# One quarter of x transposed by the DMA crossbar behind two of four FFNs, one sum of output weights by an accumulating load, and single stores, in a two-layer hybrid trunk

## The chip, the cores and the metric

The program runs on one core of one Trainium2 chip. The metric is the device time of one execution in microseconds (us), the median of three; lower is better.

## The reference

x is 512 x 1024 in float32. Two layers are run over it, each an FFN with weight 1/2, a mixer, and a second FFN with weight 1/2, and each behind an RMSNorm; a last RMSNorm gives the output. The first layer's mixer is recurrent (convolution, gates, a scan), the second's is a chunked spatial gating unit.

```python
def swiglu(x, w_in, w_out):
    g, u = jnp.split(x @ w_in, 2, axis=-1)          # w_in 1024 x 5632
    return (jax.nn.silu(g) * u) @ w_out             # w_out 2816 x 1024

h = x
for i in range(DEPTH):                               # DEPTH = 2
    h = h + 0.5 * swiglu(rms_norm(h, ffn1_norm[i]), ffn1_w_in[i], ffn1_w_out[i])
    h = h + mixer_i(rms_norm(h, mix_norm[i]))
    h = h + 0.5 * swiglu(rms_norm(h, ffn2_norm[i]), ffn2_w_in[i], ffn2_w_out[i])
return rms_norm(h, final_norm)
```

The program's order is thus FFN 1, recurrent mixer, FFN 2, FFN 3, spatial mixer, FFN 4, final norm.

## The kernel before, in words

**Products.** Every large matrix product is done in seven block products in place of eight (P1, P2, P5, P6, P3, P7, Q4: Strassen's scheme in Winograd's form). The left matrix is cut into quarters A11, A12, A22, A21, and the products take these and their sums S1 to S4 (`LEFT` names which). Each float32 operand is split into a high and a low part (`hi`, `lo`, for weights `whi`, `wlo`): ScalarE (ACT) copies the high part, VectorE (DVE) subtracts it from the value, and TensorE (PE) makes three matmuls, high by high, low by high and high by low (L465 to L467).

**Steps.** The list `subs` holds one entry for each product and each chunk of its inner dimension, some 570 in all. The last loop of `trunk` goes through them in order; at step i it splits the weights of step i+3 (`Sub.split`, L176 on), runs what was hooked to step i (`hook(n, phase, fn)`; the phases in order are pre, mid, rest, then the step's matmuls, then end and late), issues loads of weights (`load_more`) and issues the step's matmuls. A full step has 12 matmuls of 128 x 512. All engines work through their instructions in this written order, each at its own pace.

**Weights.** A load goes out on SP's queue (L140) into one of ten buffers (`raw`). Where a product needs a sum of two blocks of weights, the second block is either loaded into a buffer of its own (`tile`) and added by VectorE (`tt(self.raw.v, ...)`, in `Sub.add`), or added by an accumulating DMA on POOL's queue (`Raw.add`, L143). `Sub(..., then=block)` asks for such an accumulating load right behind the split, so that a later product finds the next sum in the same buffer. In an FFN's output products (`out_blocks` with `chain=True`), the products P1, P5, P6 and Q4 of a chunk share one buffer in this way. Before the change P6's own sum is always made with a second buffer and VectorE.

**The order of an FFN's output products** is the table `CHAIN`: 42 steps, product and chunk, such as `P25 P54 P62 Q40 Q41 P63 P55 P64 Q42 Q43 P65`. Chunk 0 has one block row of weights (128 x 512, six matmuls), chunks 1 to 5 have two.

**The norm behind an FFN.** When the last P2 is done, the quarter A11 of x (rows 0 to 255, columns 0 to 511) has its final value, and `BlockNorm.quarter("A11")` is called at that step, n. It squares the quarter for the mean, and it brings the quarter's four blocks of columns, in two groups of two, into transposed form for the next product. Before the change this is `Group.stage`: at the end of step n+2 eight 128 x 128 transposes run on TensorE (L276, `e<-ident,x`, four a group), then ScalarE takes each group out of PSUM with the norm's gain as the scale (two 128 x 256 copies), and the group is split into hi and lo (one 128 x 512 ACTIVATE, one 128 x 512 TENSOR_TENSOR). The A12, A22 and A21 quarters follow later in the same way. `BlockNorm.rest` hooks the sums S2, S4, S3 to the next product's first steps.

**The crossbar.** `Group.send` (L306 on) transposes the FFN's inner activations without TensorE: ScalarE writes the float32 values as two 16-bit planes (`pl`, two ACTIVATEs), SP issues one DMA transpose (L317), and ScalarE merges the two transposed planes into float32 (`a<-dt`, one ACTIVATE). `Group.rows` (L385 on) is the same for a quarter of x; it keeps the gains apart (`self.gain`), so that later steps multiply by them. Before the change nothing calls it.

**The end.** `FinalNorm` scales the last tiles of x and stores them. Row tiles 2 and 3 are stored together, one DMA of 512 KB per half of the columns (L1114), row tiles 0 and 1 singly (L1116).

Of the kernel before, what the change touches and what calls it, by code (L numbers as in the profile page):

```python
# [14 lines left out]
P = 128  # L15
# [10 lines left out]
V_F1, V_MIX, V_F2, V_CW, V_CB, V_GA, V_GX, V_LAM, V_SB = 0, 16, 32, 48, 80, 88, 96, 104, 112  # L26
# [31 lines left out]
def trunk(ctx: ExitStack, tc: tile.TileContext, a: dict, out: bass.AP):  # L58
    nc = tc.nc
# [19 lines left out]
    def bank(name="ps"):  # L79
        return mmp.tile([P, 512], F32, tag="mm", name=nm(name))  # L80
# [130 lines left out]
    def raw_of(src, shape, *plus):  # L211
        raws.append(Raw(src, shape, *plus))
        return raws[-1]
# [25 lines left out]
    X = cp.tile([P, TT, D], F32, tag="x", name="x")  # L239
# [178 lines left out]
    def seven(block, cuts, left, w, posts, order=None, own=False, apart=False, joined=None, opening=None,  # L418
              also=None, chain=False):

        bk, raw, held = {}, {}, []  # L430
        banks = dict(BANK, Q4=("Q", True)) if apart else BANK

        def mm_of(prod, ci):
            name, fresh = banks[prod]
            pairs = cuts[ci]

            def mm(sub):
                if fresh and ci == 0:
                    for s in range(2):
                        bk[name, s] = bank(name)[:, :w]  # L440
                if prod == joined and ci == len(cuts) - 2:
                    held.extend((sub, q, i) for q, i in enumerate(pairs))
                    return
                if opening and prod == "P1":
                    qs = list(enumerate(pairs))
                    for n, (q, i, m, s) in enumerate([(q, i, m, s) for q, i in qs for m in range(3) for s in range(2)]
                                                     if ci == 0 else
                                                     [(q, i, m, s) for m in range(3) for q, i in qs for s in range(2)]):
                        if n == (4 if ci else 6):
                            opening[ci]()  # L450
                        nc.tensor.matmul(bk[name, s], left(prod, i, s)[m == 1], (sub.lo if m == 2 else sub.hi)[:, q, :],
                                         start=(i, m) == (0, 0), stop=(i, m) == (cuts[-1][-1], 2))
                    for s in range(2 * ci):
                        posts[prod](s, bk[name, s])
                    return
                for s in range(2):
                    ps = bk[name, s]
                    k = {} if fresh else dict(skip_group_check=True)
                    if prod == joined and also is not None and ci == len(cuts) - 1:
                        also(s, ps)  # L460
                    for sb, q, i in (held if prod == joined else []) + [(sub, q, i) for q, i in enumerate(pairs)]:
                        zh, zl = left(prod, i, s)
                        wh, wl = sb.hi[:, q, :], sb.lo[:, q, :]
                        end = i == cuts[-1][-1]
                        nc.tensor.matmul(ps, zh, wh, start=fresh and i == 0, stop=False, **k)  # L465
                        nc.tensor.matmul(ps, zl, wh, start=False, stop=False, **k)  # L466
                        nc.tensor.matmul(ps, zh, wl, start=False, stop=end, **k)  # L467
                    if ci == len(cuts) - 1 and prod in posts:
                        posts[prod](s, ps)
            return mm  # L470

        kept = (0, 1) if joined else (0, 1, 2)
        order = order or [(p, ci) for p in ORDER for ci in range(len(cuts))]

        def far(ci):
            return own and order.index(("P6", ci)) - order.index(("P5", ci)) >= 4

        def again(ci):
            return own and order.index(("P5", ci)) - order.index(("P1", ci)) >= 6

        for prod, ci in order:
            if opening and (prod, ci) == ("P5", 0):
                opening[2]()

            def new(k, n, plus=None, wait=2):
                b = lambda k, n: block(k, n, cuts[ci])
                return raw_of(b(k, n), [P, len(cuts[ci]), w], plus and b(*plus), wait)

            tile = then = tile_then = None
            if chain:  # L490
                if prod == "P1" and ci in kept:
                    r, then = new(0, 0), block(0, 1, cuts[ci])
                    raw[11, ci] = r
                elif prod == "P5" and ci in kept:
                    r = raw[11, ci]
                elif prod in ("P1", "P2"):
                    r = new(int(prod == "P2"), 0)
                elif prod == "P5":
                    r = raw[11, ci] = new(0, 0, (0, 1))
                elif prod == "P6":  # L500
                    r, tile, then = raw[11, ci], new(1, 1), block(1, 0, cuts[ci])
                elif joined and prod == "P7" and ci in (4, 5):
                    r, tile = new(0, 1), new(1, 1)
                    raw[33, ci] = tile
                elif joined and prod == "P3" and ci in (4, 5):
                    r = raw[33, ci]
                elif joined and prod in ("P3", "P7"):
                    r = new(1, 1) if prod == "P3" else new(0, 1, (1, 1))
                elif prod == "P3":
                    r, then = new(1, 1), block(0, 1, cuts[ci])  # L510
                    raw[33, ci] = r
                else:
                    r = raw[33 if prod == "P7" else 11, ci]
            elif prod == "P1":
                r = raw[11, ci] = new(0, 0)
                if again(ci):
                    then = block(0, 1, cuts[ci])
            elif prod == "P2":
                r = new(1, 0)
            elif prod == "P5":  # L520
                if again(ci):
                    pass
                elif own:
                    raw[11, ci] = new(0, 0, (0, 1))
                    if far(ci):
                        then = block(1, 1, cuts[ci])
                else:
                    tile = raw[12, ci] = new(0, 1)
                    tile_then = block(1, 1, cuts[ci])
                r = raw[11, ci]  # L530
            elif prod == "P6" and far(ci):
                r, then = raw[11, ci], block(1, 0, cuts[ci])
            elif prod == "P6":
                r, tile, then = raw[11, ci], new(1, 1), block(1, 0, cuts[ci])
                raw[22, ci] = tile
            elif prod == "P3":
                r = new(1, 1) if far(ci) else raw[22, ci]
            elif prod == "P7":
                r = raw[12, ci] if not own else new(0, 1, (1, 1), 2 + ci if far(ci) else 2)
            else:  # L540
                r = raw[11, ci]
            subs.append(Sub(r, mm_of(prod, ci), None, tile, then, tile_then))
        return order


    def xt(t, n):
        return X[:, t, n * 512 : (n + 1) * 512]
# [169 lines left out]
    def out_blocks(w, k0, groups, scale, norm=None, order=None, own=False, soon={}, swap=False, p2_lag=0, chain=False, rows=None):  # L717
# [71 lines left out]
        def q4(s, ps):  # L789
# [3 lines left out]
            if not ends:  # L793
                final(2 + s, 0, "A21", s)

        at0, ends = len(subs), hasattr(norm, "last")
        order = seven(block, cuts, left_of(lambda: [gs[i] for i in range(len(n))]), 512,
                      dict(P1=p1, P2=p2, P5=p5, P6=p6, P3=p3, P7=p7, Q4=q4), order, own, True,
                      "P3" if ends else None, also=norm.gather if ends else None, chain=chain)
# [243 lines left out]
    class FinalNorm:  # L1043
# [63 lines left out]
            self.store(t, n, queue)  # L1107

        def store(self, t, n, queue=None):
            c = slice(n * 512, (n + 1) * 512)  # L1110
            if t == 2:
                return
            if t == 3:
                nc.sync.dma_start(out=out[0, 2 * P :, c].rearrange("(t p) c -> p t c", p=P), in_=X[:, 2:, c])  # L1114
                return
            (queue or nc.sync).dma_start(out=out[0, t * P : (t + 1) * P, c], in_=xt(t, n))  # L1116

        def piece(self, t, n):
            at = now[0]
# [447 lines left out]
    last = FinalNorm()  # L1567
    ffn(a["ffn1_w_in"][0], a["ffn1_w_out"][0], TileNorm(V_MIX))
    recurrent(a["rec_w_in"][0], a["rec_w_out"][0], BlockNorm(V_F2, True, wait=("A12",)))
    ffn(a["ffn2_w_in"][0], a["ffn2_w_out"][0], BlockNorm(V_F1 + 8, True))  # L1570
    ffn(a["ffn1_w_in"][1], a["ffn1_w_out"][1], BlockNorm(V_MIX + 8, True))
    spatial(a["sg_w_in"][0], a["sg_w_out"][0], BlockNorm(V_F2 + 8, True, late=True, wait=("A22",)))
    ffn(a["ffn2_w_in"][1], a["ffn2_w_out"][1], last)
    hook(len(subs) - 40, "late", last.load)
# [202 lines left out]
```

## Time and profile before

| what | value |
|---|---|
| median of 3 runs | 1564.46 us (1564.36 to 1564.46) |
| the profiled execution's own time | 1564.85 us |
| its span in the profile | 1563.1 us |
| TensorE busy | 1555.5 us, 7317 matmuls |
| VectorE busy | 1309.0 us |
| ScalarE busy | 1180.0 us |
| POOL (GpSimd) busy | 242.2 us |
| granted TensorE clock | 0.999 |
| read from HBM | 282.39 MB, 182 GB/s over the span |

The span counts from the program's first to its last instruction; the profiled execution's own time is 1.8 us more. The chain of waits is the list of pieces, each of which had to end before the next could begin, followed back from the end. A row of the timeline gives the start and the length of an instruction, its engine, line and tiles, and in brackets how long the engine had stood idle before it and for whom. A row of the view by windows gives each engine's busy time in a stretch, the granted clock, the mean busy share of the 16 DMA engines and the GB/s.

### The profile page before, as it was taken

Reading aid. Unit: us, or ns where it says so; the run is one execution under the profiler, and the core shown is the slowest. Engines: PE = TensorE matmul, PEld = TensorE weight load, DVE = VectorE, ACT = ScalarE, POOL = GpSimd, SP = SyncE. Lnnn points to the kernel's source line nnn. Section 1 sums busy time; section 2 is a strip of 40 time slices with the busy share of each in tenths; the row PEclk is TensorE's granted clock in tenths of the full one; section 3 lists DMA queues with packets and bytes.
Section 4 is the critical chain, followed back from the end, with each engine's and each line's share of the span. In section 5 each row is a group of like instructions: output and inputs, shape, how many; then the busy total and the mean of one; then the engine's idle time right before and its main releaser. Section 6 shows DMA issues by size and latency. Waiting matters only on the chain.

```text
span 1563.1 us, 21027 instructions
## 1 busy us (share of the span) xinstructions
PE 1555.5 (100%) x7317; PEld 1321.1 (85%) x7317; DVE 1309.0 (84%) x1771; ACT 1180.0 (75%) x1765; POOL 242.2 (15%) x217
## 2 busy tenths in 40 slices
PE   9999999999999999999999999999999999999998
PEld 7888888898888998888889988888888889888886
DVE  6977789978999877789887877898878997777998
ACT  7877886658778868886677788876786877778856
POOL 2111112200020111112211111122211111111120
PEclk9999999999999999999999999999999999999999
DMA  9888899943396888889978788989877869888994
GB/s 315 187 189 196 188 222 229 221 136 107 106 226 144 190 195 200 201 212 231 226 178 183 192 203 189 223 224 228 222 190 201 202 136 218 196 212 188 232 235 133
DMA packets 262426, 308.95 MB, mean 198 GB/s; under 512 B 104896, under 2 KB 142896, under 8 KB 262320
## 3 DMA queue, kind: packets, MB, share of 16 engines
q1 hardware_dynamic: 208464, 209.23, 45.6%
q0 software_dynamic: 52064, 96.54, 36.6%
q10 hardware_dynamic: 1792, 1.84, 0.5%
q8 instruction: 57, 0.93, 0.2%
q14 instruction: 49, 0.40, 0.1%
HBM read 282.39 MB, written 2.10 MB: 182 GB/s over the span
## 4 chain that ended last, share of the span: by engine, by line
PE 100%; DVE 0%; ACT 0%; issue 0%
PE A L465 15%; PE A L466 15%; PE A L467 15%; PE C L466 9%; PE C L465 8%; PE C L467 8%; PE B L466 4%; PE B L465 4%; PE B L467 4%; PE r L232 2%; PE r L231 2%; PE r L230 2%; PE Q L467 2%; PE Q L465 2%; PE Q L466 2%; PE p L939 1%
## 5 line engine op out<-in xcount | busy, mean ns | idle before, releaser
L92 DVE TENSOR_TENSOR wlo<-raw,whi 128x1024 fp32r<-128x1024 f32 (+2 forms) x567 | 651.2, 1152 | 211.1 <-ACT whi L101 204.3
L101 ACT ACTIVATE whi<-raw 128x1024 fp32r<-128x1024 f32 (+2 forms) x567 | 564.6, 1001 | 248.8 <-DVE raw L92 87.6
L465 PE MATMUL A<-whi,hi 128*128 128x512 f32 (+1 forms) x1104 | 421.0, 381 | 0.0
L467 PE MATMUL A<-wlo,hi 128*128 128x512 f32 (+1 forms) x1104 | 419.4, 380 | 0.0
L466 PE MATMUL A<-whi,lo 128*128 128x512 f32 (+1 forms) x1104 | 419.3, 380 | 0.0
L465 PEld LDWEIGHTS A<-whi,hi 128*128 128x128 f32 x1104 | 207.3, 188 | 35.9 <-ACT c L101 0.9
L467 PEld LDWEIGHTS A<-wlo,hi 128*128 128x128 f32 x1104 | 207.3, 188 | 35.7
L466 PEld LDWEIGHTS A<-whi,lo 128*128 128x128 f32 x1104 | 207.3, 188 | 35.3 <-DVE lo L92 0.3
L465 PE MATMUL C<-whi,hi 128*128 128x512 f32 (+1 forms) x608 | 231.5, 381 | 0.0
L466 PE MATMUL C<-whi,lo 128*128 128x512 f32 (+1 forms) x608 | 231.4, 381 | 0.0
L467 PE MATMUL C<-wlo,hi 128*128 128x512 f32 (+1 forms) x608 | 231.3, 380 | 0.0
L143 POOL DMA_DIRECT2D raw<-in_ffn_w_in_dram x100 | 120.8, 1210 | 710.2 <-DVE raw L92 270.8
L92 DVE TENSOR_TENSOR raw<-raw,raw 128x1024 f32<-128x1024 f32 (+2 forms) x116 | 132.8, 1145 | 1.1
L466 PEld LDWEIGHTS C<-whi,lo 128*128 128x128 f32 x608 | 114.2, 188 | 20.3 <-DVE lo L92 0.6
L465 PEld LDWEIGHTS C<-whi,hi 128*128 128x128 f32 x608 | 114.2, 188 | 19.9
L467 PEld LDWEIGHTS C<-wlo,hi 128*128 128x128 f32 x608 | 114.1, 188 | 20.0
L143 POOL DMA_DIRECT2D raw<-in_ffn_w_out_dram x70 | 81.2, 1186 | 320.6 <-DVE wlo L92 192.5
L92 DVE TENSOR_TENSOR lo<-a,hi 128x512 fp32r<-128x512 f32 (+1 forms) x188 | 121.7, 654 | 0.8 <-ACT hi L101 0.7
L101 ACT ACTIVATE hi<-a 128x512 fp32r<-128x512 f32 (+1 forms) x188 | 110.8, 596 | 14.2 <-DVE a L92 12.8
L466 PE MATMUL B<-whi,lo 128*128 128x512 f32 (+1 forms) x304 | 115.8, 381 | 0.0
L465 PE MATMUL B<-whi,hi 128*128 128x512 f32 (+1 forms) x304 | 115.7, 381 | 0.0
L467 PE MATMUL B<-wlo,hi 128*128 128x512 f32 (+1 forms) x304 | 115.6, 380 | 0.0
(185 smaller groups left out, 1919.9 us busy)
## 6 DMA issues: line engine op xcount, KB each, us to landing
raw<-in_ffn_w_in_dram SPq DMA_DIRECT2D x143, 512.0 KB, 5.6
raw<-in_ffn_w_out_dram SPq DMA_DIRECT2D x98, 512.0 KB, 5.6
raw<-in_ffn_w_in_dram POOLq DMA_DIRECT2D x76, 512.0 KB, 7.5
raw<-in_ffn_w_out_dram POOLq DMA_DIRECT2D x58, 512.0 KB, 8.3
raw<-in_ffn_w_in_dram SPq DMA_DIRECT2D x48, 384.0 KB, 4.9
raw<-in_sg_w_in_dram SPq DMA_DIRECT2D x20, 512.0 KB, 7.9
raw<-in_ffn_w_in_dram POOLq DMA_DIRECT2D x24, 384.0 KB, 6.5
raw<-in_rec_w_in_dram SPq DMA_DIRECT2D x16, 512.0 KB, 5.1
```

Source lines behind the costliest of these rows:

```text
L92: nc.vector.tensor_tensor(out=o, in0=x, in1=y, op=op)
L101: nc.scalar.activation(out=o, in_=x, func=f, **k)
L143: nc.gpsimd.dma_start(out=self.v, in_=src, accum_op=ALU.add)
L230: nc.tensor.matmul(ps, wh, xh, start=start, stop=False)
L231: nc.tensor.matmul(ps, wh, xl, start=False, stop=False)
L232: nc.tensor.matmul(ps, wl, xh, start=False, stop=stop)
L465: nc.tensor.matmul(ps, zh, wh, start=fresh and i == 0, stop=False, **k)
L466: nc.tensor.matmul(ps, zl, wh, start=False, stop=False, **k)
L467: nc.tensor.matmul(ps, zh, wl, start=False, stop=end, **k)
L939: nc.tensor.matmul(bank_of(half, s), z, (sub.lo if m == 2 else sub.hi)[:, q, :], start=left[2] == "2" and (h, q, m) == (0, 0, 0), stop=lef ...
```

## The change

Three edits are made at once.

1. The norms behind FFN 2 and FFN 3 get `cross={"A11": ...}`. The quarter A11 then goes by `Group.rows` in place of `Group.stage`: planes and DMA transpose at steps n+2 and n+3 behind FFN 2 (n+1 and n+2 behind FFN 3), the merge at steps n+6 and n+7, the split behind the merge with the gains (two 128 x 256 ACTIVATEs and two 128 x 256 SCALAR_TENSOR_TENSORs a group). The sum S2 of the next product then is two 128 x 256 SCALAR_TENSOR_TENSORs a group with the gain (`nvec`), in place of one 128 x 512 TENSOR_TENSOR.
2. In the output products of FFN 1, 2 and 3, P6's sum in chunk 0 is made by an accumulating load that follows P5's split (`then`), and no longer by a load into a second buffer and an addition on VectorE.
3. Row tiles 2 and 3 of the output are stored singly.

```diff
+        added = () if joined else (0,)
         kept = (0, 1) if joined else (0, 1, 2)
...
                 elif prod == "P5":
                     r = raw[11, ci] = new(0, 0, (0, 1))
+                elif prod == "P6" and ci in added:
+                    r, then = raw[11, ci], block(1, 0, cuts[ci])
                 elif prod == "P6":
                     r, tile, then = raw[11, ci], new(1, 1), block(1, 0, cuts[ci])
...
+            if chain and prod == "P5" and ci in added:
+                then = block(1, 1, cuts[ci])
             subs.append(Sub(r, mm_of(prod, ci), None, tile, then, tile_then))
...
         def store(self, t, n, queue=None):
-            c = slice(n * 512, (n + 1) * 512)
-            if t == 2:
-                return
-            if t == 3:
-                nc.sync.dma_start(out=out[0, 2 * P :, c].rearrange("(t p) c -> p t c", p=P), in_=X[:, 2:, c])
-                return
-            (queue or nc.sync).dma_start(out=out[0, t * P : (t + 1) * P, c], in_=xt(t, n))
+            (queue or nc.sync).dma_start(out=out[0, t * P : (t + 1) * P, n * 512 : (n + 1) * 512], in_=xt(t, n))
...
-    ffn(a["ffn2_w_in"][0], a["ffn2_w_out"][0], BlockNorm(V_F1 + 8, True))
-    ffn(a["ffn1_w_in"][1], a["ffn1_w_out"][1], BlockNorm(V_MIX + 8, True))
+    ffn(a["ffn2_w_in"][0], a["ffn2_w_out"][0], BlockNorm(V_F1 + 8, True, cross={"A11": (((2, "mid"), (6, "mid"), (6, "rest")), ((3, "mid"), (7, "mid"), (7, "rest")))}))
+    ffn(a["ffn1_w_in"][1], a["ffn1_w_out"][1], BlockNorm(V_MIX + 8, True, cross={"A11": (((1, "mid"), (6, "mid"), (6, "rest")), ((2, "mid"), (7, "mid"), (7, "rest")))}))
     spatial(a["sg_w_in"][0], a["sg_w_out"][0], BlockNorm(V_F2 + 8, True, late=True, wait=("A22",)))
```

The first place is PE's order between steps P62 and Q40 of FFN 2's output products (`A` and `Q` are banks of PSUM, `e` the transposed blocks of x). Before:

```order
L466 MATMUL A_6560<-whi_6906,lo_6913 128x512
L467 MATMUL A_6560<-wlo_6907,hi_6912 128x512
L276 MATMUL e_7002<-ident,x 128x128 x4
L276 MATMUL e_7007<-ident,x 128x128 x4
L465 MATMUL Q_7033<-whi_6928,hi_6932 128x512
L466 MATMUL Q_7033<-whi_6928,lo_6933 128x512
```

And after the change:

```order
L466 MATMUL A_6558<-whi_6902,lo_6909 128x512
L467 MATMUL A_6558<-wlo_6903,hi_6908 128x512
L465 MATMUL Q_7019<-whi_6924,hi_6928 128x512
L466 MATMUL Q_7019<-whi_6924,lo_6929 128x512
L467 MATMUL Q_7019<-wlo_6925,hi_6928 128x512
```

The eight transposes are gone; nothing else of PE's order has moved, here or behind FFN 3.

The second place is ACT at steps n+6 and n+7 (P55 and P64) of the same output products, where the planes are merged; these steps split the weights of Q43 and P65. Before (`whi` is a split of weights, `hi` one of activations, a pair for each step):

```order
L101 ACTIVATE whi_7090<-raw_6625 128x1024
L101 ACTIVATE hi_7094<-a_1325_6211 128x512
L101 ACTIVATE whi_7116<-raw_6762 128x1024
L101 ACTIVATE hi_7121<-a_1408_6576 128x512
L101 ACTIVATE whi_7137<-raw_6892 128x512
```

And after:

```order
L101 ACTIVATE whi_7072<-raw_6601 128x1024
L101 ACTIVATE hi_7076<-a_1324_6209 128x512
L101 ACTIVATE a_1526_7080<-dt_6987 128x1024
L101 ACTIVATE hi_7082<-a_1526_7080,vec 128x256 x2
L101 ACTIVATE whi_7106<-raw_6758 128x1024
L101 ACTIVATE hi_7111<-a_1407_6574 128x512
L101 ACTIVATE a_1535_7115<-dt_7013 128x1024
L101 ACTIVATE hi_7117<-a_1535_7115,vec 128x256 x2
L101 ACTIVATE whi_7135<-raw_6888 128x512
```

A merge and two half splits now stand between the splits of weights, twice. The two take-outs and the split of each group, which stood four steps earlier, are gone from there, and the planes stand in their place.

The third place is DVE in the first steps of the spatial mixer, where S2 (`a<-s,a`) is made. Before:

```order
L92 TENSOR_TENSOR a_2155_9991<-s_2285_10557,a_2155_9991 128x512
L92 TENSOR_TENSOR raw_10303<-raw_10303,raw_10359 128x1024
L92 TENSOR_TENSOR wlo_10625<-raw_10281,whi_10624 128x1024
L92 TENSOR_TENSOR c_2293_10582<-c_2293_10582,B_10608 128x512
L92 TENSOR_TENSOR c_2294_10590<-c_2294_10590,B_10609 128x512
L92 TENSOR_TENSOR a_2158_9998<-s_2286_10560,a_2158_9998 128x512
L92 TENSOR_TENSOR wlo_10645<-raw_10303,whi_10644 128x1024
L92 TENSOR_TENSOR lo_10650<-a_2155_9991,hi_10649 128x512
```

And after:

```order
L98 SCALAR_TENSOR_TENSOR a_2172_10052<-a_2172_10052,nvec,s_2286_10557 128x256 x2
L92 TENSOR_TENSOR raw_10303<-raw_10303,raw_10359 128x1024
L92 TENSOR_TENSOR wlo_10626<-raw_10281,whi_10625 128x1024
L92 TENSOR_TENSOR c_2294_10582<-c_2294_10582,B_10608 128x512
L92 TENSOR_TENSOR c_2295_10590<-c_2295_10590,B_10609 128x512
L98 SCALAR_TENSOR_TENSOR a_2181_10087<-a_2181_10087,nvec,s_2287_10560 128x256 x2
L92 TENSOR_TENSOR wlo_10647<-raw_10303,whi_10646 128x1024
L92 TENSOR_TENSOR lo_10652<-a_2172_10052,hi_10651 128x512
```

Each of the two sums has become two instructions of half the width; the order around them is the same.

## The prediction, as it was made before the run

> **What bounds the kernel now.** I read the page's busy times first, then its chain of waits.
>
> ```profile
> PE 1555.5 (100%) x7317; PEld 1321.1 (85%) x7317; DVE 1309.0 (84%) x1771; ACT 1180.0 (75%) x1765; POOL 242.2 (15%) x217
> ...
> PE 100%; DVE 0%; ACT 0%; issue 0%
> ```
>
> TensorE is never without work, and the chain of waits is TensorE from the opening to the last 5 us. So the end moves by what is taken from TensorE's own list, and by any new pause in it. Behind comes the question how far the engines that feed it are ahead. In the output products of FFN 2 they have little to spare (view by windows):
>
> ```profile
> 729.30:734.60 5.30, 5.30 (x29) 4.46 (x28) 5.30 (x7) 4.65 (x9) 1.20 (x1) 1.00 1.05 327
> 734.60:740.50 5.90, 5.90 (x28) 4.89 (x27) 5.90 (x9) 4.39 (x8) 1.21 (x1) 1.00 0.94 203
> 740.50:746.00 5.50, 5.50 (x26) 4.56 (x25) 5.02 (x7) 3.85 (x6) 0.00 (x0) 1.00 1.01 251
> 746.00:751.40 5.40, 5.40 (x26) 4.46 (x25) 4.68 (x7) 2.63 (x5) 3.17 (x3) 1.00 0.67 187
> ```
>
> The columns are length, PE, PEld, DVE, ACT, POOL, clock, DMA share and GB/s. PE is full in each; VectorE too until 740.5, and the DMA engines are near 1.0 for 17 us. So each edit has to be followed to the moment at which TensorE needs its result.
>
> **Part 1a: what TensorE loses.** The chain in order of time has the transposes of A11 behind FFN 2 and FFN 3:
>
> ```profile
> 731.76 0.24 PE A L467
> 731.99 0.87 PE e L276 x8
> 732.87 0.23 PE Q L465
> ...
> 1051.07 0.87 PE e L276 x8
> ```
>
> Eight transposes cost the chain 0.87 us, between matmuls of 0.23 us. Both groups go: 2 x 0.87 = **1.74 us less**.
>
> **Part 1b: what ScalarE and VectorE get instead, in the output products.**
>
> ```profile
> L101 ACT ACTIVATE pl<-c 128x512 uint16<-128x512 uint16 x160 | 88.2, 620 | 4.9 <-DVE c L98 3.0 <-DVE c L92 1.5
> L101 ACT ACTIVATE a<-dt 128x1024 uint16<-128x1024 uint16 x60 | 70.4, 1173 | 0.0
> L101 ACT ACTIVATE a<-e,vec 128x256 f32<-128x256 f32 x55 | 22.3, 470 | 0.6 <-DVE lo L98 0.6
> L101 ACT ACTIVATE hi<-a 128x256 fp32r<-128x256 f32 x20 | 8.0, 402 | 0.0
> L98 DVE SCALAR_TENSOR_TENSOR s<-e,vec,a 128x256 f32<-128x256 f32 x20 | 8.3, 476 | 4.0 <-PE e L276 4.0
> L92 DVE TENSOR_TENSOR a<-s,a 128x512 f32<-128x512 f32 x32 | 21.5, 682 | 0.0
> ```
>
> For a group, ScalarE loses two take-outs (2 x 0.47) and a split of about 0.62 (the planes' row, same width), 1.6 us; it gets two planes (2 x 0.62), a merge (1.17) and two half splits (2 x 0.40), 3.2 us. The planes take about the place of the work that goes, four steps earlier; the merge and the half splits, 1.97 us, are new at the two steps that split the weights of Q43 and P65. VectorE loses a 0.68 us subtraction and gets two of 0.48 there. What does that do to TensorE? The timeline:
>
> ```profile
> 733.18 1.20 POOL L143 DMA_DIRECT2D raw<-in_ffn_w_out_dram  x1 [6.14 <-DVE wlo L92]
> 742.15 1.07 ACT L101 ACTIVATE whi<-raw 128x1024 fp32r<-128x1024 f32 x1 [3.15 <-DMA raw<-in_ffn_w_out_dram]
> 743.63 1.05 ACT L101 ACTIVATE whi<-raw 128x1024 fp32r<-128x1024 f32 x1
> 744.99 1.28 DVE L98 SCALAR_TENSOR_TENSOR x<-C,x 128x512 f32<-128x512 f32 x2
> 747.32 0.68 DVE L92 TENSOR_TENSOR lo<-a,hi 128x512 fp32r<-128x512 f32 x1
> 750.63 0.39 PE L466 MATMUL A<-whi,lo 128*128 128x512 f32 x1
> ```
>
> This is the tightest place. ScalarE waits 3.15 us for an accumulating load, then everything follows in a row. With the change, merge and half splits start at 743.63 and the next split of weights at 745.6 in place of 743.63. VectorE gets its two half subtractions at 745.2 (the first half's hi), is through at 746.0, updates x until 747.2 and takes the next weights' low part until 748.4; the `lo` at 747.32 then ends at about 749.0 in place of 748.0. TensorE reads it at 750.63, or 0.87 earlier without the transposes, 749.76. **0.8 us of 2.6 are left**, no pause; cost 0. If that cover were gone, each further 0.1 us would be 0.1 us of the end. Later steps gain on this, since ScalarE is idle half of 746 to 751.4.
>
> **Part 1c: SP's queue and the DMA engines.** Each transpose is one more instruction on SP, ahead of the loads written behind it. Of the view by line, all transposes; then the landings of L143's accumulating loads from 726 to 760 us; then the same from 676 to 690 us, where transposes run beside them:
>
> ```profile
> L317 SPq DMA_TRANSPOSE dt<-pl x96: 1197/1252/2284, 46.1 to 1456.6; - x96
> ...
> DMA to landing us min/median/max: 2.4/3.6/7.8
> ```
>
> ```profile
> DMA to landing us min/median/max: 5.7/8.3/10.0
> ```
>
> ```profile
> DMA to landing us min/median/max: 5.7/5.7/5.9
> ```
>
> A transpose holds SP for 1.25 us and lands 3.6 us after issue, 7.8 at worst. The merge comes four steps of 2.7 us (12 matmuls of 0.23) later, so 7.8 is in time. The loads behind the pair are delayed some 2.5 us, and such a delay has room (view of waits):
>
> ```profile
> ACT whi L101 <- DMA raw<-in_ffn_w_out_dram: 12.4, 4, 4.0
> ```
>
> In the whole run ScalarE waited four times for output weights to land, of all its splits. The one at 742.15 is such a time, and its load is an accumulating one, issued at 733.18, while the transposes would be moving. Beside transposes such loads landed in 5.7 to 5.9 us, without them here in 5.7 to 10.0, so I take no delay; for the range I keep the worst of 10.0 (1.0 us more than the 9.0 from 733.18 to 742.15, 0.2 of it past the cover) and the pair's whole DMA time. That time is read from a stretch with one pair and hardly anything else:
>
> ```profile
> 566.10:570.90 4.80, 4.80 (x26) 4.37 (x25) 3.29 (x5) 4.32 (x7) 0.00 (x0) 1.00 0.46 94
> ```
>
> 0.46 x 4.8 = 2.2 us of all 16 engines.
>
> **Part 1d: S2 with a gain.** In FFN 3 and in the spatial mixer S2 becomes two 0.48 us instructions in place of one of 0.68. In the spatial mixer:
>
> ```profile
> 1112.80 1.66 DVE L98 SCALAR_TENSOR_TENSOR s<-e,vec,a 128x256 f32<-128x256 f32 x4 [1.52 <-PE e L276]
> 1125.95 0.68 DVE L92 TENSOR_TENSOR lo<-a,hi 128x512 fp32r<-128x512 f32 x1
> 1126.80 0.40 PE L466 MATMUL A<-whi,lo 128*128 128x512 f32 x1
> ...
> 1131.46 0.68 DVE L92 TENSOR_TENSOR lo<-a,hi 128x512 fp32r<-128x512 f32 x1
> 1132.26 0.43 PE L466 MATMUL C<-whi,lo 128*128 128x512 f32 x1
> ```
>
> The first row has four such halves in 1.66 us, so one starts (1.66 - 0.48) / 3 = 0.40 us after another, 0.08 before the one ahead ends; by the same overlap a whole takes 0.60. That is 0.79 for 0.60, 0.19 us more, twice. From 1112.80, where VectorE waited for TensorE, it has no pause up to the `lo` that ends at 1126.63; TensorE reads that at 1126.80. With 0.38 us more the lead of 0.17 becomes -0.21, and the next tight one, 1132.14 for 1132.26, gives 0.05 more (TensorE comes 0.21 later, the lead is 0.12, ScalarE's part of the chain is 0.38 later too): **0.26 us of pause**. Bounds: 0 (were two halves as cheap as one whole) to 0.6 (0.38 at each of the two places, less 0.12). In FFN 3 a pause of VectorE comes first:
>
> ```profile
> 813.39 1.23 DVE L92 TENSOR_TENSOR wlo<-raw,whi 128x1024 fp32r<-128x1024 f32 x1 [0.56 <-ACT whi L101]
> ```
>
> Its 0.56 us take up the 0.38, so 0 there; without it up to 0.4.
>
> **Part 2: the accumulating load in place of an addition.** VectorE loses three additions of 0.68 us, off TensorE's list: 0. The wait moves from SP's load to POOL's. FFN 2 again:
>
> ```profile
> 699.69 1.20 POOL L143 DMA_DIRECT2D raw<-in_ffn_w_out_dram  x1 [14.95 <-DVE x L98]
> 707.26 0.63 ACT L101 ACTIVATE whi<-raw 128x512 fp32r<-128x512 f32 x1 [2.40 <-DVE raw L92]
> 713.82 0.68 DVE L92 TENSOR_TENSOR lo<-s,hi 128x512 fp32r<-128x512 f32 x1
> 715.73 0.39 PE L466 MATMUL C<-whi,lo 128*128 128x512 f32 x1
> ```
>
> ScalarE splits P60's weights at 707.26, after 2.40 us of waiting for the addition. In POOL's order the new load stands behind the one at 699.69, and that one's own load is written one place earlier, since one buffer fewer is taken. With the load at 699.69 where it was, the new one starts at 700.9 and lands, at the median of 8.3, at 709.2: 1.9 us after 707.26, against a lead of 1.23 us at the next tight read (714.50 for 715.73) and 0.6 us of VectorE time that is freed: pause 0 to 0.7. With it one step of 2.7 us earlier, as one load fewer ahead of it makes likely, the new one lands at 706.5, in time. I take 0.
>
> **Part 3: single stores.**
>
> ```profile
> 1554.17 0.90 SPq L1114 DMA_DIRECT2D out_dram<-x  x2
> 1556.90 2.55 SPq L1116 DMA_DIRECT2D out_dram<-x  x3
> ```
>
> Four stores in place of two, 0.4 us each to issue, are through before SP's next at 1556.90, which waits for the last tiles: 0, with 0.1 either way.
>
> **Sum.** -1.74 + 0.26 = -1.48 us. Against the profiled execution's own 1564.85 that is 1563.37; it ran 0.39 us above the median of the runs shown, 1564.46, so I predict **1563.0**, with 1562.5 to 1563.5 as the forecast's own range (pauses of 0 to 0.7, and 0.2 of scatter). A measurement can tell about 0.2%, 3.1 us, from no change, so this is inside "the same".
>
> **Rivals.**
> - *DMA time decides* (slower). The two transposes' 2.2 us go ahead of the accumulating load that Q43's weights wait for. Past the 0.8 us cover that is a pause of 1.4 us, behind both FFNs 2.8: 1563.0 + 2.8 = 1565.8, slower than before. It decides from 1.5 us of pause on. For it: the DMA share near 1.0, the wait of 3.15 us. Against it: 5.7 to 5.9 us beside transposes. Chance 0.13.
> - *P60's accumulating load is late*: up to 0.7 us in three FFNs, 1563.0 to 1565.1. For it: its place behind another load on POOL. Against it: that load's earlier start. Chance 0.12.
> - *TensorE's saving is not the end's*: VectorE, full from 729 to 740 us, sets the pace, and the 1.74 us become pauses: 1564.7. Against it: TensorE's leads of microseconds there. Chance 0.08.
> - *The crossbar is slow.* If it took four steps and more, the merge would hold ScalarE, and each microsecond past the 0.8 would be one of the end: with landings of 15 us in place of 7.8, 15 - 10.8 - 0.8 = 3.4 us a norm, 1563.0 + 6.8 = 1569.8. The rows say 2.4 to 7.8. The Trainium skill's page "VectorE: DVE Perf Modes" ("The three transpose paths") speaks for it, and against this change: it gives 1309 ns by the crossbar and 390 ns on TensorE for a 128 x 128 block, and advises TensorE where PSUM will do as a target. By that, as an estimate, a group's eight blocks take 10.5 us. This trace disagrees, with 3.6 us for eight. Chance 0.02.
>
> **How the numbers follow.** Forecast 0.6; rivals 0.13, 0.12, 0.08, 0.02; 0.05 for what I don't see. 8 in 10 need the forecast, the late load, the lost saving and a share of the first rival: 1562.4 to 1565.2. Faster by over 0.2% (below 1561.3) has no mechanism, 0.02; slower by over 0.2% (above 1567.6) is the slow crossbar and part of the unseen, 0.06; the same, 0.92.
>
> **What would show it.** Eight transposes fewer at the two places, and TensorE's neighbours there 0.23 us apart; the accumulating load before Q43 landing within 10 us, and TensorE without a gap before P65; a gap of some 0.2 us before the first S2 read of the spatial mixer; P60's split by 708 us. A gap at P65 would make the first rival right; leads shrunk by 0.87 us without a shorter span, the third.

## The result, and the profile after

The changed kernel takes 1567.29 us (median of 19 executions, 1565.17 to 1571.84), the kernel before 1564.80 us (19 executions, 1564.36 to 1565.46): a ratio of 1.0019, interval 1.0012 to 1.0026. It is 2.5 us slower, where 1.5 us less was predicted, and above the predicted range. New too is a scatter of 6.7 us from one execution to the next, where before had 1.1. The profiled execution took 1566.24 us, 1.39 more than that of before.

TensorE still bounds the kernel, but a piece of the chain of waits has left it (page of the changed kernel, then three pieces of the chain in order of time: start, length, what):

```profile
PE 1554.4 (99%) x7301; PEld 1318.6 (84%) x7301; DVE 1308.9 (84%) x1776; ACT 1186.7 (76%) x1773; POOL 245.2 (16%) x220
PE 94%; DMA 2%; DVE 2%; issue 1%; ACT 0%; POOL 0%; SPq 0%; POOLq 0%; DVEq 0%; ACTq 0%
```
```profile
1051.24 12.47 DMA raw<-in_ffn_w_out_dram
1063.82 1.06 ACT whi L101
1065.40 1.08 ACT a L101
```

The 16 transposes are gone (7317 matmuls are 7301). In their place the chain holds an accumulating load of POOL's queue behind FFN 3, issued at 1051.24, 12.47 us long, and behind it ScalarE's split of Q43's weights and the first merge. The next view shows who was waiting (timeline of the changed kernel, POOL's issue, ScalarE's split, and the three matmuls of TensorE that start late):

```profile
1051.24 1.20 POOL L143 DMA_DIRECT2D raw<-in_ffn_w_out_dram  x1 [6.67 <-DVE lo L92]
...
1063.82 1.06 ACT L101 ACTIVATE whi<-raw 128x1024 fp32r<-128x1024 f32 x1 [7.90 <-DMA raw<-in_ffn_w_out_dram]
...
1065.45 0.49 PE L465 MATMUL Q<-whi,hi 128*128 128x512 f32 x1 [0.37 <-ACT hi L101]
1066.79 0.50 PE L466 MATMUL Q<-whi,lo 128*128 128x512 f32 x1 [0.85 <-DVE lo L92]
1070.91 0.50 PE L466 MATMUL A<-whi,lo 128*128 128x512 f32 x1 [1.11 <-DVE lo L92]
```

The same split in the kernel before:

```profile
1060.95 1.06 ACT L101 ACTIVATE whi<-raw 128x1024 fp32r<-128x1024 f32 x1 [2.88 <-DMA raw<-in_ffn_w_out_dram]
```

ScalarE stood 7.90 us for that load, 2.88 in before. TensorE is late at Q43 (twice) and at P65. Matmuls start 0.23 us apart; these three start 0.76, 1.34 and 1.49 us after the one ahead, 2.90 us too late in all, and the matmul behind each of the last two is another 0.11 us late: 3.1 us. The rest of the balance is -1.74 us for the transposes and +0.38 us in the spatial mixer (below): about +1.8 us in all. TensorE's last matmul starts 1.7 us later than before (1558.10 for 1556.41). What follows it took 0.3 us less, so that the execution is 1.39 us longer.

The view by windows shows what the load met (length, PE, PEld, DVE, ACT, POOL, clock, DMA share, GB/s; changed kernel, behind FFN 3):

```profile
1054.00:1056.00 2.00, 2.00 (x10) 1.65 (x9) 2.00 (x4) 1.61 (x3) 0.49 (x1) 1.00 1.29 216
1056.00:1058.00 2.00, 2.00 (x11) 1.65 (x10) 2.00 (x3) 0.00 (x0) 0.71 (x1) 1.00 2.04 113
1058.00:1060.00 2.00, 2.00 (x11) 1.65 (x10) 1.28 (x2) 0.00 (x0) 0.00 (x0) 1.00 0.85 64
1060.00:1062.00 2.00, 2.00 (x11) 1.65 (x10) 0.00 (x0) 0.00 (x0) 0.00 (x0) 1.00 1.08 257
```

From 1056 to 1060 us the DMA engines are busy at a share of 2.04 and then 0.85, and move 113 and then 64 GB/s. Before had there:

```profile
1056.00:1058.00 2.00, 2.00 (x11) 1.65 (x10) 2.00 (x4) 2.00 (x4) 0.21 (x1) 1.00 1.09 223
1058.00:1060.00 2.00, 2.00 (x11) 1.65 (x10) 2.00 (x3) 0.07 (x1) 1.01 (x1) 1.00 0.77 230
```

The packets of POOL's queue in these 4 us (packets, MB, share of the 16 engines; before, then changed):

```profile
q0 software_dynamic: 201, 0.38, 57.5%
```
```profile
q0 software_dynamic: 89, 0.18, 114.3%
```

Share times 16 engines times 4 us, over the packets, is 0.18 us for a packet before and 0.82 us after: the engines are not out of work, their packets take longer. Below, "collapse" means such a stretch. While it lasts ScalarE and then VectorE run dry.

### The profile page after: what moved, and what is told of

It reads as the page before. It is cut to its first block, busy times and chain, and to the rows that moved or that the text cites. A ratio compares the mean times of both kernels' runs of the same rounds, so it can differ in the third digit from the quotient of the medians.

```text
span 1564.5 us, 21022 instructions
## 1 busy us (share of the span) xinstructions
PE 1554.4 (99%) x7301; PEld 1318.6 (84%) x7301; DVE 1308.9 (84%) x1776; ACT 1186.7 (76%) x1773; POOL 245.2 (16%) x220
## 4 chain that ended last, share of the span: by engine, by line
PE 94%; DMA 2%; DVE 2%; issue 1%; ACT 0%; POOL 0%; SPq 0%; POOLq 0%; DVEq 0%; ACTq 0%
PE A L466 15%; PE A L467 15%; PE A L465 15%; PE C L466 8%; PE C L467 8%; PE C L465 8%; PE B L466 4%; PE B L467 4%; PE B L465 4%; PE r L231 2%; PE r L232 2%; PE r L230 2%; PE p L944 1%; PE Q L467 1%; PE Q L466 1%
## 5 line engine op out<-in xcount | busy, mean ns | idle before, releaser
L92 DVE TENSOR_TENSOR raw<-raw,raw 128x1024 f32<-128x1024 f32 (+1 forms) x113 | 130.9, 1158 | 1.1
L101 ACT ACTIVATE hi<-a 128x512 fp32r<-128x512 f32 (+1 forms) x184 | 108.5, 595 | 14.4 <-DVE a L92 12.6
```

The source lines that it names most:

```text
L92: nc.vector.tensor_tensor(out=o, in0=x, in1=y, op=op)
L101: nc.scalar.activation(out=o, in_=x, func=f, **k)
```

## The experiments

**Theory A**: transposes in flight beside POOL's accumulating load slow both, and Q43's weights come late. **Theory B**: it is ScalarE's added work (merge, half splits) ahead of P65. **Theory C**: part 2's accumulating load moves the plain loads into a collision. The number behind each "before" is the kernel before on the same chip.

**The parts alone.** e1, part 1:

```diff
-        added = () if joined else (0,)
+        added = ()
```
(and the stores as before). 

> Part 1 of the change alone (both quarters by the crossbar, P6's sum and the stores as before). Theory A: a crossbar transpose in flight delays the accumulating load that Q43's weights wait for, mostly behind FFN 3, and TensorE pauses before P65; then this shows the whole loss, 1567.3 +- 1 us with the same scatter of several us from one execution to the next, and a gap of some 3 us at Q43/P65. Theory C: the accumulating load of part 2 frees a buffer, pulls the plain loads a step earlier and so makes the collision; then this gives the forecast, 1563 to 1564 us, with a scatter below 1 us.

Measured: 1566.18 us (12 executions; before 1564.76; ratio 1.0012, 1.0001 to 1.0023). Four executions took 1562.77 to 1563.66, the other eight 1564.4 to 1571.3. The four reach the time forecast, 1563.0, so my reading is that part 1 gives it when nothing collapses; none of the four was profiled. Part 1 alone loses 1.4 us at the median, the whole change 2.5: less of the loss than I expected of part 1. (Of the changed kernel's 19 executions none is below 1565.17.)

e2, parts 2 and 3:

```diff
-    ... BlockNorm(V_F1 + 8, True, cross={"A11": ...}))
-    ... BlockNorm(V_MIX + 8, True, cross={"A11": ...}))
+    ... BlockNorm(V_F1 + 8, True))
+    ... BlockNorm(V_MIX + 8, True))
```


> Parts 2 and 3 alone (accumulating load for P6 in chunk 0, single stores; both quarters on TensorE as before). Theory A: no difference, 1564.8 +- 0.4 us, scatter below 1 us. Theory C: part or all of the loss without any transpose, 1566 to 1567 us.

Measured: 1564.94 us (1564.29 to 1565.67; before 1564.76; 0.9992 to 1.0009). No loss and no scatter. Parts 2 and 3 alone cost nothing, and part 1 loses without it, so theory C falls as the main cause.

e3 and e4, part 1 behind one FFN (as e1, `cross` of the other FFN taken away). 

> Part 1 behind FFN 2 alone, all else as before. Theory A: 0.87 us less for the eight transposes and a landing before Q43 that is not later than before: 1563.9 +- 0.4 us, little scatter. Theory B (ScalarE's merge and half splits alone eat the cover before P65, whichever FFN): half of the loss, 1565.5 to 1566 us.

 

> Part 1 behind FFN 3 alone, all else as before. Theory A: the loss and its scatter stand here: 1567.5 us, 1565 to 1571 from one execution to the next. Theory B: as much as behind FFN 2, 1565.5 to 1566 us. Theory C: -0.87 + 0.26, 1564.2 us.

Measured: e3 1564.17 us (1563.48 to 1565.32), e4 1570.04 us (five executions, 1569.34 to 1572.55; 1.0025 to 1.0051). The loss stands behind FFN 3. It is 5.3 us in e4, more than the whole change loses: the parts do not add up, and the runs do not say why. The profiled execution of e4 shows a longer wait than that of the changed kernel (windows, POOL's load by line, ScalarE's split):

```profile
1058.00:1060.00 2.00, 2.00 (x11) 1.65 (x10) 2.00 (x3) 0.00 (x0) 0.14 (x1) 1.00 1.55 58
1060.00:1062.00 2.00, 2.00 (x11) 1.65 (x10) 0.37 (x1) 0.00 (x0) 0.00 (x0) 1.00 1.91 69
...
1070.00:1072.00 2.00, 2.00 (x7) 1.63 (x8) 1.86 (x4) 2.00 (x5) 0.00 (x0) 0.73 0.99 369
1072.00:1074.00 2.00, 2.00 (x6) 1.39 (x5) 2.00 (x4) 1.97 (x4) 0.34 (x1) 0.50 0.58 223
```
```profile
DMA to landing us min/median/max: 14.8/14.8/14.8
```
```profile
1066.92 1.06 ACT L101 ACTIVATE whi<-raw 128x1024 fp32r<-128x1024 f32 x1 [10.33 <-DMA raw<-in_ffn_w_out_dram]
```

The load takes 14.8 us, 8.6 in before. TensorE pauses 4.2 us, and then the granted clock (the third number from the right) is 0.73 and 0.50 for some 4 us: eight matmuls start about 0.43 us apart in place of 0.23, 1.6 us more. With -0.87 and +0.38 that makes 5.3 us, for 5.2 measured. The Trainium skill has a rule for this on its page "TensorE: Matmul & The Clock Gate" ("Why this matters for your kernels"): gaps of more than about 3 us between bursts of matmuls put TensorE back to half its clock. This trace agrees: the clock is 0.50 behind a pause of 2.98 us, which is at that limit, and one of 1.11 us.

**ScalarE or the DMA engines?** From here to e13, and in e16 and e17, each kernel is e4 with one thing altered. The table `cross` has, for each of the two groups of blocks, the step (counted from n) of the planes and the transpose, of the merge, and of the half splits. e5, merges later:

```diff
-  cross={"A11": (((1, "mid"), (6, "mid"), (6, "rest")), ((2, "mid"), (7, "mid"), (7, "rest")))}
+  cross={"A11": (((1, "mid"), (10, "mid"), (10, "rest")), ((2, "mid"), (11, "mid"), (11, "rest")))}
```


> As e4 (crossbar behind FFN 3 alone), with the merges and half splits at steps n+10 and n+11 in place of n+6 and n+7; planes and transposes stay. Theory A (transposes and the accumulating load hold each other up in the DMA engines): the load before Q43 still lands 12 to 15 us after issue; TensorE's pause shrinks by at most the two us of a merge and its half splits, 1567 to 1569 us. Theory B (ScalarE's own work before Q43 and P65): the pause is gone, 1564.2 us.

Measured: 1569.47 us, eight of ten executions from 1567.2 to 1571.1, two at 1563.8 and 1564.4. The loss stays when the merges move, so theory B falls as the main cause. The profiled execution was one of the two good ones: POOL's load landed in 8.6 us, with one window of 75 GB/s (share 1.46, 1052 to 1054 us). The landing in the bad ones wasn't seen.

e6 and e7, the whole transfer later: `(9, 14)` and `(10, 15)`; `(6, 11)` and `(7, 12)` in the same table (planes, merge). 

> As e4, with planes and transposes at steps n+9 and n+10 and merges at n+14 and n+15, behind the load that Q43 waits for. Theory A: that load lands in 8 to 9 us again and the pause at Q43 is gone; POOL issues accumulating loads for P3's chunks there, so the transposes may be slow, but nothing reads them for 4 steps: 1564.2 us, with a pause of a few us further on if those loads are then late for their splits. Theory B: 1564.2 us as well. A cost of the transposes wherever they stand (more DMA time in a kernel near its DMA limit): 1566 us or more.

 

> As e4, with planes and transposes at steps n+6 and n+7 and merges at n+11 and n+12: between the last of the accumulating loads before P65 and the burst of them behind it. Theory A: transposes land in 3 to 5 us, no pause, 1564.2 us. Theory B: the planes (2.5 us of ScalarE in all) stand where the merges stood, before P65's split, so part of the pause remains, 1565 to 1566 us.

Measured: e6 1570.45 us (1566.84 to 1578.06), e7 1565.93 us (1563.97 to 1570.62). I was too hopeful in both. In e6 POOL's load before Q43 is back at 8.6 us, but the transposes now stand in the burst of POOL's loads for P3's chunks; they land after 13.3 and 21.8 us, and TensorE waits once for 6.1 us:

```profile
DMA to landing us min/median/max: 13.3/17.5/21.8
```
```profile
PE A L465 <- ACT hi L101: 6.1, 1, 6.1
```

So the collapse goes with the transposes to another group of POOL's loads. In e7 the first transpose met none and landed in 3.6 us, the second met the burst and took 10.3. e7's median lies in the range of theory B (1565 to 1566), but its profiled execution (1568.54) has TensorE without a gap up to P65; its gaps come later, from 1093.7 us on.

**What do the transposes collide with?** e8 makes the load that Q43 waits for a plain one on POOL's queue, e9 puts that plain load on SP's (in each FFN, one load):

```diff
-            nc.gpsimd.dma_start(out=self.v, in_=src, accum_op=ALU.add)
+            nc.gpsimd.dma_start(out=self.v, in_=src)        # e8
+            nc.sync.dma_start(out=self.v, in_=src)          # e9
```


> As e4, with the load that Q43's weights wait for a plain one on the same queue at the same place (Q43's sum lacks its first blocks: this leaves out part of the computation). Theory A in the form that the accumulation is what the transposes collide with: the load lands in 6 to 9 us and the pause is gone, 1564.2 us. If it is only that POOL's queue and a transpose are moved at once, whatever the load does: still 12 us and more, 1568 to 1571 us.

 

> As e4 (crossbar behind FFN 3 alone), with the load that Q43's weights wait for as a plain load on SP's queue at the same place (Q43's sum lacks its first blocks: this leaves out part of the computation). Theory A2 (a transpose and a load of POOL's queue in flight together hold each other up, accumulating or not): with SP's queue alone the load lands in 5 to 8 us, the windows keep over 180 GB/s, 1564.2 us, scatter below 1.5 us. Rival D (any load beside a pair of transposes): still 12 us and 1566 to 1570.

Measured: e8 1566.36 us (1563.99 to 1567.89), e9 1564.80 us (1564.19 to 1565.41). The load's landing and ScalarE's split behind it in e8 (an execution of 1567.89 us); then the load's issue and the split in e9:

```profile
DMA to landing us min/median/max: 12.6/12.6/12.6
```
```profile
1065.00 1.06 ACT L101 ACTIVATE whi<-raw 128x1024 fp32r<-128x1024 f32 x1 [8.09 <-DMA raw<-in_ffn_w_out_dram]
```
```profile
1052.34 0.42 SPq L144 DMA_DIRECT2D raw<-in_ffn_w_out_dram  x1
...
1059.41 1.06 ACT L101 ACTIVATE whi<-raw 128x1024 fp32r<-128x1024 f32 x1 [2.46 <-DMA raw<-in_ffn_w_out_dram]
```

In e9 the load was there at most 7.1 us after its issue, since the split begins then, and no window around it is below 220 GB/s. So a collapse does not need the accumulation. That accumulation adds nothing is not shown: e8 loses 1.7 us where e4 loses 5.3, and four of its ten executions are below 1565. In e9 the collapse is gone. Its load also goes out 0.53 us ahead of the second transpose (in e8 0.04 us from it), so the queue and the order are not told apart. The Trainium skill's page "DMA: Bandwidth & Descriptors" ("Issuing engines are not separate DMA queues") says that loads share the same 16 engines whoever issues them, so the choice saves issue time alone. These two runs differ from it: 12.6 and at most 7.1 us for the same 512 KB, with the choice of queue and the 0.5 us in the order as the differences.

e10, one of the two groups by the crossbar:

```diff
-  cross={"A11": (((1, "mid"), (6, "mid"), (6, "rest")), ((2, "mid"), (7, "mid"), (7, "rest")))}
+  cross={"A11": (((1, "mid"), (6, "mid"), (6, "rest")), None)}
```


> As e4, but only the first group of two column blocks goes by the crossbar, the second by TensorE as before. Theory E (it takes two transposes in flight, the second behind a full queue): no collapse, 1564.8 - 0.44 + 0.13 = 1564.5 us with little scatter. Theory A2 (one transpose beside a load of POOL's queue is enough): the first transpose lands before that load moves (it was through after 4 us in e4), so the loss is also mostly gone, but runs of 1566 us and more remain.

Measured: 1564.55 us; nine of ten at 1563.87 to 1565.75, one at 1567.69. Most of the loss needs the second transpose. One alone still brought a window of 96 GB/s (share 1.25, 1052 to 1054 us), without a late load.

**The place.** e11: planes and merges at `(18, 21)` and `(19, 22)`. 

> As e4, with planes and transposes at steps n+18 and n+19 and merges at n+21 and n+22, where in the trace of before POOL's queue has nothing in flight (1092.3 to 1098.2 us). Theory A2: transposes land in 3 to 5 us, no window below 100 GB/s, 1564.2 us, scatter below 1 us. If the two transposes slow the loads wherever they stand: 1566 us and more.

Measured: 1566.28 us (1565.75 to 1567.25). The transposes were slower than I expected (6.0 and 8.5 us) but not the cause: TensorE now waits 1.6 us at the transposes of the quarter that follows. VectorE updates that quarter's x late, behind a split that ScalarE brought late, and on ScalarE the merges and half splits of A11 stand just ahead. A free place on the DMA engines isn't one on ScalarE.

e12: planes at n+2 and n+3, merges at n+6 and n+7, as behind FFN 2. 

> As e4, with the steps that the change uses behind FFN 2: planes at n+2 and n+3, merges at n+6 and n+7. If the place one step later is what spares FFN 2 (the load before Q43 is issued ahead of the second transpose): 1564.2 us, as behind FFN 2 alone. If FFN 2 is spared by something else: 1568 to 1570 us as in e4.

Measured: 1564.41 us (1563.88 to 1565.72), and POOL's load lands in 7.4 us. One step takes 5.6 us off the median. e4's and e12's issues (timeline, SP's queue and POOL):

```profile
1049.50 1.24 SPq L395 DMA_TRANSPOSE dt<-pl  x1
1050.84 1.05 SPq L140 DMA_DIRECT2D raw<-in_ffn_w_out_dram  x2
1052.01 2.66 SPq L395 DMA_TRANSPOSE dt<-pl  x1
...
1051.98 1.22 POOL L143 DMA_DIRECT2D raw<-in_ffn_w_out_dram  x1 [6.16 <-DVE wlo L92]
```
```profile
1046.07 4.17 SPq L140 DMA_DIRECT2D raw<-in_ffn_w_out_dram  x3
1051.47 4.51 SPq L395 DMA_TRANSPOSE dt<-pl  x2
...
1051.88 1.22 POOL L143 DMA_DIRECT2D raw<-in_ffn_w_out_dram  x1 [6.14 <-DVE wlo L92]
```

In e4 the first transpose stands on SP ahead of two plain loads, which go out at 1050.84 and 1051.5; in e12 they had gone by 1049.9. And in e4 the second transpose starts with POOL's load, in e12 2.1 us behind it. **Theory F** takes the second difference, **theory H** the first: a transpose that waits for its planes holds plain loads back, and they meet the pair and POOL's load.

e13 (planes at n+1 and n+3), e16 (both at n+2), e17 (as e4, issued by ScalarE):

```diff
+  cross={"A11": (((1, "mid"), (6, ...)), ((3, "mid"), (7, ...)))}     # e13
+  cross={"A11": (((2, "mid"), (6, ...)), ((2, "mid"), (7, ...)))}     # e16
-                nc.sync.dma_start_transpose(out=d[0]...)
+                nc.scalar.dma_start_transpose(out=d[0]...)            # e17
```


> As e4 (crossbar behind FFN 3 alone), with the second group's planes and transpose at n+3 in place of n+2; the first stays at n+1. Theory F (the collapse comes when the second transpose is issued within some 0.3 us of POOL's load): the load moves ahead of it and lands in 7 to 9 us, 1564.3 us, scatter below 2 us. Rival G (the first transpose has to be issued right before POOL's load, as in e12, not 2 us before): still 1568 us and more.

 

> As e4 (crossbar behind FFN 3 alone), with both transposes at step n+2, 1.3 us apart, merges at n+6 and n+7. If the second transpose's nearness to POOL's load decides (theory F): collapse, median 1566 us and more or executions up to 1570. If it is the plain loads held back behind the first transpose (rival H): 1564.3 us, scatter below 2 us, as e12.

 

> As e4 (crossbar behind FFN 3 alone, planes at n+1 and n+2, merges at n+6 and n+7), with the two transposes issued by ScalarE in place of SP. Theory H (the first transpose, waiting on SP's queue for its planes, holds two plain loads back so that they meet the pair and POOL's load): the plain loads are issued at 1048.7 and 1049.9 again, POOL's load lands in 7 to 9 us, 1564.3 us, at most 1 us more if ScalarE's time for the issue (about 1.25 us each) is missed. Theory F (nearness of the second transpose to POOL's load): collapse as in e4, 1568 to 1570 us.

Measured: e13 1564.71 us (nine at 1563.88 to 1565.9, one at 1568.75), e16 1564.69 us (1564.01 to 1566.30), e17 1567.16 us (1565.93 to 1569.30). In e16 the second transpose comes 0.94 us behind POOL's load, without harm. In e17 it comes 0.03 us behind it (rows below: the issues on ScalarE's queue, then POOL's), and the load lands in 8.7 us, with windows of 127 and 71 GB/s (share 0.67 in the second). In that execution F does not hold. e17's loss is another: each issue holds ScalarE 1.3 us ahead of splits that TensorE soon needs, and TensorE's gaps there come to 3.3 us; I had allowed 1.

```profile
1051.46 1.32 ACTq L395 DMA_TRANSPOSE dt<-pl  x1
...
1055.54 1.26 ACTq L395 DMA_TRANSPOSE dt<-pl  x1
...
1055.51 1.22 POOL L143 DMA_DIRECT2D raw<-in_ffn_w_out_dram  x1 [10.01 <-DVE wlo L92]
```

H fits these executions of e4, e12, e16 and e17, but e17 moved POOL's load 3.5 us later as well. Three profiled executions go against it: e13 (one window of 73 GB/s, 1052 to 1054 us), e5 and e1 have plain loads held back as e4 has, and POOL's load lands in 8.3 to 8.6 us. e1 behind FFN 3, SP's queue and POOL, then the landing:

```profile
1050.94 1.23 SPq L395 DMA_TRANSPOSE dt<-pl  x1
1052.26 1.06 SPq L140 DMA_DIRECT2D raw<-in_ffn_w_out_dram  x2
1053.45 1.83 SPq L395 DMA_TRANSPOSE dt<-pl  x1
...
1053.42 1.22 POOL L143 DMA_DIRECT2D raw<-in_ffn_w_out_dram  x1 [6.49 <-DVE wlo L92]
```
```profile
DMA to landing us min/median/max: 8.6/8.6/8.6
```

The order is that of e4, and the second transpose comes 0.03 us behind POOL's load in both; yet e4's load took 14.8 us. So neither F nor H decides a single execution. The step shifts how often a collapse comes; what tips one stays open.

**The change, mended.** e14 is part 1 alone, e15 the whole change, both with n+2 and n+3 behind FFN 3 too:

```diff
-    ... BlockNorm(V_MIX + 8, True, cross={"A11": (((1, "mid"), ...), ((2, "mid"), ...))}))
+    ... BlockNorm(V_MIX + 8, True, cross={"A11": (((2, "mid"), ...), ((3, "mid"), ...))}))
```


> Part 1 of the change alone, with the steps n+2, n+3, n+6, n+7 behind both FFNs. Theory F: -0.6 (e3) and -0.35 (e12) add up, 1563.8 us, most executions 1563.0 to 1564.5, few above 1566. If these steps collapse now and then by themselves (e1's execution): a median of 1564 to 1565 with executions up to 1568.

 

> The whole change, with FFN 3's steps n+1, n+2 replaced by n+2, n+3. If the place alone made the loss: 1563.8 us as e14, within 0.4. If parts 2 and 3 shift the loads into the transposes: 1565 us and more, scatter of several us.

Measured: e14 1563.82 us (1562.73 to 1564.99), e15 1563.25 us (1562.84 to 1565.22; before 1564.64; ratio 0.9993, 0.9984 to 1.0002). With one step moved, the median of the whole change comes to the time forecast, and the scatter falls to 2.4 us. The gain against before, 1.4 us, is not shown: the interval includes no change.

## Why the prediction was wrong, step by step

- **1a, TensorE's loss of work: right.** The 16 transposes left the chain, and times that fit the 1.74 us come back: e15 with 1563.25, e1's four lowest executions with 1562.8 to 1563.7.
- **1b, ScalarE's work before P65 costs nothing: right as far as the load comes in time.** e12 and e15 have merge and half splits at the same steps and no pause there; e5 shows that moving them doesn't help. Where the load is late, the third late matmul of the changed kernel stands behind the merge and its half splits.
- **1c, "so I take no delay" for the accumulating load before Q43: this step failed.** The term was put at nothing. Behind FFN 3 the load came 12.5 us after issue (e4: 14.8), where 8.6 had been, and TensorE lost 3.1 us. The prediction followed this wait behind FFN 2, where the changed kernel's load did land in 7.4 us; behind FFN 3, where the transposes stand one step earlier, it followed no row. I had compared with the loads at 676 to 690 us, "beside transposes". The timeline of before shows that for the most part they were not:

```profile
674.89 2.61 SPq L317 DMA_TRANSPOSE dt<-pl  x2
...
686.71 2.76 SPq L317 DMA_TRANSPOSE dt<-pl  x2
...
677.45 0.90 POOL L143 DMA_DIRECT2D raw<-in_ffn_w_out_dram  x1 [15.50 <-DVE wlo L92]
680.59 1.20 POOL L143 DMA_DIRECT2D raw<-in_ffn_w_out_dram  x1 [2.24 <-DVE wlo L92]
683.54 1.20 POOL L143 DMA_DIRECT2D raw<-in_ffn_w_out_dram  x1 [1.74 <-DVE wlo L92]
```

  The first pair had landed by 680.0, the second left at 686.7. So the first load overlapped a pair for its first 2.5 us, the third for its last 2.6 us, and the middle one none. A stretch with real overlap was there, 650 to 657 us (two transposes from 649.5, POOL's loads issued at 650.3 and 652.6; landings of the transposes, of the loads, and a window):

```profile
DMA to landing us min/median/max: 3.1/5.2/7.4
```
```profile
DMA to landing us min/median/max: 6.8/8.2/9.6
```
```profile
652.00:654.00 2.00, 2.00 (x11) 1.65 (x10) 1.97 (x3) 2.00 (x4) 1.20 (x1) 1.00 0.85 88
```

  88 GB/s at a share of 0.85, a second transpose of 7.4 us and a load of 9.6: a mild collapse stood in the trace of before.
- **1d, S2 with a gain: right in the mechanism, a little small in size.** 0.26 us were forecast, 0.21 at the first read and 0.05 at a second place. The A matmul below comes 0.50 us behind the one ahead, 0.27 late, with its `lo` from VectorE; the one behind it is another 0.11 late, and the second place adds nothing: 0.38 us, within the bounds of 0 to 0.6.

```profile
1127.72 0.68 DVE L92 TENSOR_TENSOR lo<-a,hi 128x512 fp32r<-128x512 f32 x1
...
1127.96 0.39 PE L465 MATMUL A<-whi,hi 128*128 128x512 f32 x1
1128.46 0.50 PE L466 MATMUL A<-whi,lo 128*128 128x512 f32 x1
```

- **Parts 2 and 3 cost nothing: right**, by e2, but with little to spare. P60's split came at 708.42, 0.4 us after the 708 forecast and 1.16 us later than before, and no matmul waited: the lead of 1.23 us just covered it.
- **The rivals.** "DMA time decides" had the right wait and the right victim, at a chance of 0.13, but the wrong price: I charged the pair's own 2.2 us, once behind each FFN. In truth the engines' throughput falls to about a third, which costs the load 3.9 to 6.2 us, and almost only behind FFN 3. "The crossbar is slow" is not what cost the changed kernel its time: its transposes behind FFN 3 took 4.2 and 9.5 us, and nothing waited for them. In the trace of before, transposes with no load of POOL's in flight land in 2.4 to 5.7 us, and e7's first in 3.6. But beside POOL's loads they can be as slow as that rival feared: in e6 one took 21.8 us, and ScalarE waited 7.5 us for it. The other two fall by e2 and e15.
- **The range** had bounded the load's delay by a worst row of 10.0 us, taken from places without transposes. That the ratio, 1.0019, lies within the 0.2% called "the same" is luck: a loss stands there in place of a gain.

Open: why the engines lose their throughput with transposes and POOL's loads in flight together, what part the order on SP's queue has, and why the same program collapses in one execution and not in the next. In its profiled execution e1 collapsed behind FFN 2 (POOL's loads of 10.9 and 15.0 us), at the steps at which those of e3, e14 and e15 did not, and although the plain loads had gone out ahead of the pair:

```profile
738.00:740.00 2.00, 2.00 (x11) 1.65 (x10) 2.00 (x4) 0.16 (x1) 0.97 (x1) 1.00 2.13 67
```

## What to carry to other kernels

Moving work to the DMA engines in a stretch where they are near full is priced by the latest load that somebody waits for, not by the bytes: find a row in which both kinds are really in flight together, from both issue times and both landings, before using it as evidence. An instruction that waits on an issuing queue holds back all loads written behind it, so a step more or less changes what meets what, and here it changed how often the loss came; try the neighbouring steps. Look at the scatter of the executions too: here it told of the fault before any trace.

## What the runs showed of the hardware

- Two crossbar transposes with POOL's and SP's loads in flight brought the DMA engines from some 200 to 380 GB/s down to 73 for 2 us (e13) and to 58, 69 and 93 for 6 us (e4), at shares of 0.84 to 1.91; e6's transposes took 13.3 and 21.8 us.
- The same program spread over 8.5 us (e1, 1562.77 to 1571.32) with nothing changed from one execution to the next.
- A plain load of 512 KB took 12.6 us on POOL's queue beside the pair, and at most 7.1 on SP's, 0.5 us ahead of the second transpose. A packet of POOL's queue took 0.82 us beside the pair (after), 0.18 without it (before).
- Behind pauses of 2.98 and 1.11 us (e4) TensorE's granted clock fell to 0.50 and cost another 1.6 us.
